# A two-layer hybrid DiT block in one core: layer 1's GLA level scores issued ahead of its SSD scans, modulation steps beside the levels, and an FFN opening that begins on the first half of the tokens

## The chip, the cores and the metric

The kernel runs on one core of a Trainium2 chip. The metric is the device time of one execution in microseconds (us); lower is better. The core has a matrix engine (TensorE, in the profile PE, with its weight loads as PEld), a vector engine (VectorE, DVE), an activation engine (ScalarE, ACT), a general engine (GpSimd, POOL) and a queue that issues DMAs (SyncE, SP). Each engine works off its own instructions in order; they wait for one another by semaphores.

## The reference, cut to what matters

The input is 512 latent tokens and 256 context tokens of width 1024. Two layers follow; each mixes tokens by three head groups side by side and then applies a SwiGLU FFN. A modulation vector (shift, scale, gate, for the mixer and for the FFN) comes from a matrix `ada_w` of 1024 x 6144 per layer.

```python
for l in range(DEPTH):                                  # DEPTH = 2
    last = l == DEPTH - 1
    mod_l = (silu(c) @ ada_w[l] + ada_b[l])             # six vectors: sh1, sc1, gt1, sh2, sc2, gt2
    p_l = modulate(rms_norm(lat, norm_mix_pre[l]), sh1, sc1) @ w_in[l]
    p_c = ...                                           # the same for the context
    gla_c, gla_l = gla_mixer(...)                       # gated linear attention, decay per key channel
    ssd_c, ssd_l = ssd_mixer(...)                       # causal conv, then Mamba-2 scans
    ret_c, ret_l = retention_mixer(...)                 # rotary retention, fixed decay per head
    mixed_l = concatenate([gla_l, ssd_l, ret_l]) @ w_out[l]
    lat = lat + gt1 * rms_norm(mixed_l, norm_mix_post[l])
    h_l = modulate(rms_norm(lat, norm_ffn_pre[l]), sh2, sc2)
    lat = lat + gt2 * rms_norm(swiglu(h_l, ffn_w13[l], ffn_w2[l]), norm_ffn_post[l])
    # the context goes through the same, but not behind the mixer of the last layer
```

All scans run in both directions; the latents start from the states at the end of the context. In layer 1 only the 512 latent tokens leave the mixer.

## The kernel before, in words

**Arithmetic.** Every large product is made of three fp32r matmuls: each operand is split into a high part (a cast on ACT, line 368) and a low part (a subtraction on DVE, line 369), and hi*hi, hi*lo and lo*hi are added up in PSUM. Tokens are worked on in blocks of 128: blocks 0 to 3 are latents, 4 and 5 context.

**Order.** The program is written in order, and a planner then lays out each engine's instructions: earlier program order goes first among those that its own timing holds ready, `tc.high_priority(offset=n)` moves a region ahead by n instructions. So work whose operands come early can run ahead of its place, as far as its tiles have memory. Tiles live in pools on a left and a right stack; a pool opened after another was closed lies over its memory, and a tile then waits until the tiles under it are done (`reuse_waits="tile"`). PSUM has eight banks: `mm` (2) for projections, `px` (5) for everything else, `pa` (1) for the modulation.

**A layer, in program order.**
- Projections of the small columns (gates, dt) and the gate chain in pool `Sa` (lines 664 to 744), which leaves the cumulated GLA gates `GG`; then the convolutions, eight blocks `fb` of 128 channels with their projections (lines 746 to 780): the conv's tiles `acc`, `th` and `xf` are in pool `Sc`, opened before `Sa`.
- The SSD scans in pool `Sb` (lines 782 to 872), at high priority: `ssd_state` and `ssd_out`, mostly DVE work. They read `CB` and `xs`, the first tiles of pool `S` on the left stack.
- The projection `gqk` of GLA's q and k (lines 873 to 880), then `rk`, `rq`, `rv` (`proj_b`, line 613).
- Retention and GLA: pools `Q` and `R` on the right, `G` and `Gl` on the left (lines 971 to 973), over pool `S`. `gla_prep` (975) makes the decayed keys and queries; `gla_levels` (1004) makes the score matrix `A` of 256 tokens level by level, for seven block sizes: subtractions on DVE and POOL (1016 to 1019), an exponential on ACT (1020), a product on DVE (1021), 8 short matmuls (1028), and four masked copies on DVE (1035). `pump` (1113) issues one piece of retention (`ret_kv`, `ret_out`) behind a level. `ret_out` holds its transposed operands in one buffer (`rqT`, line 934).
- The GLA states and outputs (`gla_kv`, `gla_step`, `gla_out`, from line 1152), the projections `gr`, `rg`, `z0`, `z1`, and the output projection by block: `out_front` (1194) normalizes, gates, transposes and multiplies with `w_out`; `out_back` (1237) adds the residual and makes the FFN's input `whole`.
- The FFN's first product by Strassen's scheme on four quarters of `whole` (`b11`, `b12` are the upper 512 features of the first and second half of the tokens, `b21`, `b22` the lower ones). Its **opening** (lines 1293 to 1370) splits `b11` and `b21`, makes the sums t1 to t4, and begins NA units (3 in layer 0, 4 in layer 1) with the two products that need `b11` and `b21` alone; then `ffn_up` (1334) works off 22 units, each with weights that are loaded, combined (417 to 420) and split.
- The FFN's second product, `down` (1387), in two passes.

**Modulation.** `Ada` (line 250) is a list of steps; a step loads 512 KB of `ada_w` into `araw` (NRAW = 3 buffers, pool `adp`) and makes 4 matmuls into `pa`; every eighth step ends one of the six vectors. `ada.some(n)` issues n steps. Layer 0 has 48 steps (32 of its own, 16 for layer 1's first two vectors), layer 1 has 32. They are issued behind `rq` (6), behind `rv` (8), in each `gla_out` (4), and what is left behind the last `out_back`.

## Time and profile before

| | |
|---|---|
| time, median of 3 runs | 1884.56 us (1883.4 to 1886.07) |
| the profiled execution, its own time | 1887.56 us |
| its span, first to last instruction | 1885.8 us |
| mean granted clock of TensorE | 0.954 of full speed |
| TensorE busy | 1748.4 us, 93% of the span |
| VectorE, ScalarE, GpSimd busy | 62%, 42%, 31% |
| HBM read and written | 233.72 MB and 38.93 MB, 145 GB/s |

The profile shows one execution, 1.9 us apart from its span and 3.0 us above the median of the timed runs. Engine busy times can overlap; a share is of the whole span. The granted clock is given as a share of full speed (2.4 GHz; the other level is 1.2 GHz, 0.50). "Idle before, releaser" names what an engine last waited for.

### The profile page before, as it was taken

The page shows a single profiled execution, that of the slowest core. Times are in us where ns is not written, and L with a number is a line of the kernel's source. Part 1 is how long each engine was busy: PE and PEld are TensorE (multiplying, and loading weights), DVE is VectorE, ACT ScalarE, POOL GpSimd, SP SyncE. Part 2 cuts the span into 40 slices and gives each one's busy share as a digit, 9 for nine tenths or more (in the row PEclk, how much of TensorE's full clock was granted, in tenths as well). Part 3 has the DMA queues.
Part 4 walks back from the last instruction along what each step waited for, and adds up shares of the span by engine and source line. Part 5 has one row for each costly group of instructions (what it writes and reads, how often), then busy time and mean ns, then how long its engine had stood idle before and what let it go on. Part 6 is the DMA issues. An engine that isn't in the chain of part 4 may idle for free. (4 is left out here: it accounts for less than half of the span.)

```text
span 1885.8 us, 30347 instructions
## 1 busy us (share of the span) xinstructions
PE 1748.4 (93%) x11851; PEld 1580.3 (84%) x11851; DVE 1164.4 (62%) x1967; ACT 791.5 (42%) x1439; POOL 592.5 (31%) x584
## 2 busy tenths in 40 slices
PE   5999999999969999999999989989977879999998
PEld 3778889988859999998788777889866879999886
DVE  4576778656467655564333528677855468888445
ACT  3545344235553433332333555534423444444343
POOL 1002624114244433231422320162313236555322
PEclk8999999999979999999999899999958979999999
DMA  8535464138534333332744473445315145444653
GB/s 280 180 103 171 139 186 132 49 112 291 176 102 132 109 107 109 93 93 97 258 142 165 133 234 122 120 145 188 103 51 185 68 129 145 130 140 129 244 201 136
DMA packets 238189, 274.63 MB, mean 146 GB/s; under 512 B 14041, under 2 KB 181437, under 8 KB 238045
## 3 DMA queue, kind: packets, MB, share of 16 engines
q1 hardware_dynamic: 236832, 270.77, 44.8%
q8 instruction: 93, 1.52, 0.3%
q10 hardware_dynamic: 1212, 1.91, 0.3%
q14 instruction: 52, 0.42, 0.1%
HBM read 233.72 MB, written 38.93 MB: 145 GB/s over the span
## 5 line engine op out<-in xcount | busy, mean ns | idle before, releaser
L369 DVE TENSOR_TENSOR wlo<-raw,whi 128x1024 fp32r<-128x1024 f32 (+2 forms) x192 | 264.2, 1382 | 162.3 <-ACT whi L368 162.1
L1316 PE MATMUL px<-H,whi 128*128 128x384 f32 (+1 forms) x1408 | 309.7, 312 | 9.2 <-ACT whi L368 9.0
L368 ACT CAST whi<-raw 128x1024 fp32r<-128x1024 f32 (+2 forms) x192 | 194.1, 1018 | 236.0 <-PE px L1316 88.0
L498 PE MATMUL mm<-whi,H 128*128 128x256 f32 x1376 | 272.2, 293 | 13.3 <-ACT stg L630 6.7
L1316 PEld LDWEIGHTS px<-H,whi 128*128 128x128 f32 x1408 | 236.8, 191 | 11.2 <-ACT whi L368 11.1
L498 PEld LDWEIGHTS mm<-whi,H 128*128 128x128 f32 x1376 | 223.0, 196 | 24.9 <-ACT stg L630 9.5
L1316 PE MATMUL px<-H,wlo 128*128 128x384 f32 (+1 forms) x704 | 212.4, 311 | 0.8 <-DVE wlo L369 0.8
L498 PE MATMUL mm<-wlo,H 128*128 128x256 f32 x688 | 200.4, 291 | 0.0
L498 PE MATMUL mm<-H,whi 128*128 128x256 f32 (+2 forms) x640 | 160.9, 342 | 4.0 <-ACT xp L759 3.6
L368 ACT CAST whi<-S 128x1024 fp32r<-128x1024 f32 x88 | 73.6, 836 | 163.1 <-DVE S L419 91.5
L498 PEld LDWEIGHTS mm<-wlo,H 128*128 128x128 f32 x688 | 134.8, 196 | 1.4
L1316 PEld LDWEIGHTS px<-H,wlo 128*128 128x128 f32 x704 | 132.2, 191 | 2.0 <-DVE wlo L369 2.0
L1271 POOL TENSOR_TENSOR hidlo<-hr,hidhi 128x768 fp32r<-128x768 f32 (+1 forms) x40 | 71.3, 1785 | 191.1 <-ACT hidhi L1270 173.3
L498 PEld LDWEIGHTS mm<-H,whi 128*128 128x128 f32 (+1 forms) x640 | 109.5, 190 | 22.6 <-ACT xp L759 5.3
L498 PE MATMUL px<-whi,H 128*128 128x256 f32 x640 | 121.1, 288 | 5.2 <-DVE H L1230 3.7
L1357 POOL TENSOR_TENSOR hf<-hf,g 128x384 f32<-128x384 f32 (+1 forms) x44 | 56.6, 1287 | 219.8 <-issue 141.3
L369 DVE TENSOR_TENSOR wlo<-S,whi 128x1024 fp32r<-128x1024 f32 x88 | 92.2, 1048 | 41.3 <-ACT whi L368 41.1
L1316 PE MATMUL mm<-blo,whi 128*128 128x384 f32 (+1 forms) x328 | 103.2, 315 | 9.5 <-DVE blo L1291 9.5
L498 PEld LDWEIGHTS px<-whi,H 128*128 128x128 f32 x640 | 100.7, 192 | 12.6 <-DVE H L1230 5.2
L498 PE MATMUL mm<-H,wlo 128*128 128x256 f32 (+3 forms) x320 | 108.5, 339 | 0.0
L1392 PE MATMUL px<-wlo,hidhi 128*128 128x512 f32 x276 | 108.3, 393 | 0.0
L1316 PE MATMUL mm<-bhi,whi 128*128 128x384 f32 (+1 forms) x328 | 103.6, 316 | 4.2 <-ACT bhi L1290 3.3
(321 smaller groups left out, 4124.0 us busy)
## 6 DMA issues: line engine op xcount, KB each, us to landing
raw<-ffn_w_dram SPq DMA_DIRECT2D x99, 512.0 KB
araw<-ada_w_dram SPq DMA_DIRECT2D x96, 512.0 KB
raw<-w_in_dram SPq DMA_DIRECT2D x26, 1024.0 KB
raw<-ffn_w_dram SPq DMA_DIRECT2D x20, 1024.0 KB
hr<-hd SPq DMA_DIRECT2D x22, 768.0 KB
hr<-hd SPq DMA_DIRECT2D x22, 512.0 KB
Rt<-gd SPq DMA_DIRECT2D x40, 256.0 KB
hd<-hf SPq DMA_DIRECT2D x22, 384.0 KB
```

The source lines that it names most:

```text
L368: S.copy(hi, src)
L369: lo_engine.tensor_tensor(lo, src, hi.bitcast(F32), ALU.subtract)
L498: PE.matmul(ps, x(k), y(k), start=(k == 0 and p == 0), stop=(k == total - 1 and p == 2))
L1271: (G if q else V).tensor_tensor(lo[:, q], hr[:, q], hi[:, q].bitcast(F32), ALU.subtract)
L1316: PE.matmul(ps[:, :hn], w[x][:, k], r[y][:, k], start=first and k == 0 and p == 0, stop=k == 3 and p == 2, skip_group_check=True)
L1357: G.tensor_tensor(h1, h1, g1, ALU.mult)
L1392: PE.matmul(ps, lh[x](k), rh[y](k), start=f + k == 0 and p == 0, stop=f + k == NF - 1 and p == 2, skip_group_check=True)
```

## The change

The functions `gla_prep` and `gla_levels` move up in the file without a change of their arithmetic. In layer 1 (`last`) their pools `G` and `Gl` are opened at the start of the layer on the right stack, the projection `gqk` comes between the conv's blocks 5 and 6, and preparation and levels are issued behind the conv and ahead of the SSD scans; retention is then issued in one go. In layer 0 levels and retention stay in their place, and three modulation steps are issued with each level. In layer 1 the buffers of the modulation come from a pool `ar` that opens behind the scans. The rest is memory (NRAW 2, fewer buffers of `xw`, `y`, `kw`, `hr`; the conv's tiles in a pool `Sd` that opens after `Sa` is closed), a second buffer for `rqT`, and a new FFN opening: NA is 4 in both layers; `b11` is split block by block in `out_back`, into the memory of the constants (`cst2`) and of `araw`; all NA units first make their `b11` product, then their `b21` product; the sums t2 and t3 have their split tiles apart from t1 and t4; all low parts are made on DVE.

```diff
-    NRAW = 3
+    NRAW = 2
-        u["xbc"] = {j: w_unit("xbc", wi, 1312 + 256 * j, 256) for j in (2, 3, 0, 1)}
-        u["gqk"] = w_unit("gqk", wi, 0, 256)
+        u["xbc"] = {}
+        for j in (2, 3, 0, 1):
+            u["xbc"][j] = w_unit("xbc", wi, 1312 + 256 * j, 256)
+            if j == 2:
+                u["gqk"] = w_unit("gqk", wi, 0, 256)
-        NA = 3 if l + 1 < NL else 4
+        NA = 4
...
+        arp = adp
         Ms = mx.enter_context(pool(f"Ms{l}", side="right"))
+        gst = ctx.enter_context(ExitStack())
         gx = ctx.enter_context(ExitStack())
+        if last:
+            Gp = gst.enter_context(pool(f"G{l}", side="right"))
+            Gl = gx.enter_context(pool(f"Gl{l}", side="right"))
...
+                kw = pt(Gl, "kw", [128, TL], bufs=1 if last else 2)[:, :n]     # in gla_prep
...
+                if li >= start:                                                # in gla_levels
+                    pump()
+                if not last:
+                    ada.some(3)
...
-            with scx:
+            with scx, pool(f"Sd{l}") as Sd:
                 for fb in (4, 5, 6, 7, 0, 1, 2, 3):
+                    if fb == 6:
+                        un = get(u["gqk"])
...
-                    acc = pt(Sc, "acc", [128, T + 4], bufs=2)
+                    acc = pt(Sd, "acc", [128, T + 4], bufs=2)
...
+            if last:
+                gc = gla_prep(TL, TC, False)
+                gl = gla_prep(0, TL, True)
+                for t0 in (0, 256):
+                    gla_levels(t0, 99)
             with pool(f"Sb{l}") as Sb, tc.high_priority(offset=300):
...
-                    xw = pt(Sb, "xw", [128, 512], bufs=2)
+                    xw = pt(Sb, "xw", [128, 512], bufs=1 if last else 2)
-                    y = pt(Sb, "y", [128, 512], bufs=3)
+                    y = pt(Sb, "y", [128, 512], bufs=2)
...
-            un = get(u["gqk"])
...
+        if last:
+            arp = ax.enter_context(pool(f"ar{l}", 2))
+        ada.ap = arp
         proj_b("rk", tbs_all, to_dram(qds[l], 256, "rope"))
...
-            qT = pt(Rp, "rqT", [128, 4, 2, 128], bufs=1)
+            qT = pt(Rp, "rqT", [128, 4, 2, 128], bufs=2)
...
-        with tc.high_priority(offset=60):
-            gc = gla_prep(TL, TC, not last)
-            if not last:
+        if not last:
+            with tc.high_priority(offset=60):
+                gc = gla_prep(TL, TC, True)
                 gla_levels(TL, 99)
-            gl = gla_prep(0, TL, True)
-        gla_levels(0, 2)
-        gla_levels(256, 1)
+                gl = gla_prep(0, TL, True)
+            gla_levels(0, 2)
+            gla_levels(256, 1)
         gls.close()
         pump(100)
...
+        near, far = ("right", "left") if last else ("left", "right")
...
-        ada.some(len(ada.todo) - 12)
+        ada.some(len(ada.todo))
...
             pre_norm(nps, l, 2, tb, x, whole, pos)                              # in out_back
+            if pos < n2:
+                cs = slice(128 * pos, 128 * pos + 128)
+                S.copy(b11h[:, :, cs], whole[:, 0:4, cs])
+                for q in range(2):
+                    ks = slice(2 * q, 2 * q + 2)
+                    V.tensor_tensor(b11l[q][:, :, cs], whole[:, ks, cs], b11h[:, ks, cs].bitcast(F32), ALU.subtract)
...
         out_back(*prev)
-        ada.some(len(ada.todo))
         rx.close()
         mx.close()
-        ax.close()
...
-            for i in range(n2):
-                cs = slice(128 * i, 128 * i + 128)
-                rsplit("b11", whole[:, 0:4, cs], cs, V)
-                rsplit("b21", whole[:, 4:8, cs], cs, G)
+            def combine(i):
...
                 V.tensor_tensor(t1, b12, b11, ALU.subtract)
                 V.tensor_tensor(t2, b22, t1, ALU.subtract)
-                G.tensor_tensor(t3, b22, b12, ALU.subtract)
+                rsplit("t2", t2, cs)
+                V.tensor_tensor(t3, b22, b12, ALU.subtract)
+                rsplit("t3", t3, cs)
                 V.tensor_tensor(t4, b21, t2, ALU.subtract)
-            for i in range(n2):
-                cs = slice(128 * i, 128 * i + 128)
-                for nm, q in (("t2", 1), ("t3", 2), ("t1", 0), ("t4", 3)):
-                    rsplit(nm, tm[:, q, :, cs], cs, V)
-                rsplit("b22", whole[:, 4:8, hn + 128 * i:hn + 128 * i + 128], cs, G)
+                rsplit("b22", b22, cs)
...
-            begun = {}
+            begun = []
             for f in range(NA):
-                un = get(u["w13a"][f])
-                ps = [mm(), px()][f % 2]
-                uu = up_first(ps, un)
-                begun[f] = uu, up_gate(ps, un)
+                un = get(u["w13a"][f], 0)
+                ps = mm() if f < 2 else px()
+                up_first(ps, un, uus[f])
+                begun.append((ps, un))
+            for i in range(n2):
+                cs = slice(128 * i, 128 * i + 128)
+                rsplit("b21", whole[:, 4:8, cs], cs)
+            for f, (ps, un) in enumerate(begun):
+                up_gate(ps, un, g1s[f])
+            for i in range(n2):
+                combine(i)
+            tb_ = pt(hp, "H", [128, 4, 4, hn], F32R)
...
+            for q, nm in enumerate(("t1", "t4")):
+                rsplit(nm, t14[:, q], allsl)
...
         fx.close()
+        ax.close()
```

## Rows read from the trace of the kernel before

**Rows 1.** The page: busy times; TensorE's busy tenths and granted clock in 40 slices.

```profile
PE 1748.4 (93%) x11851; PEld 1580.3 (84%) x11851; DVE 1164.4 (62%) x1967; ACT 791.5 (42%) x1439; POOL 592.5 (31%) x584
...
PE   5999999999969999999999989989977879999998
...
PEclk8999999999979999999999899999958979999999
```

**Rows 2.** Windows, layer 1's mixer: busy time and count by engine, granted clock, DMA.

```profile
1216.00:1312.00 96.00, 90.89 (x714) 85.38 (x713) 75.64 (x159) 41.08 (x107) 50.64 (x63) 0.98 0.52 158
1312.00:1360.00 48.00, 47.22 (x428) 44.00 (x427) 38.45 (x89) 18.66 (x43) 16.61 (x28) 1.00 0.48 155
1360.00:1412.00 52.00, 39.65 (x245) 33.76 (x244) 28.81 (x78) 15.08 (x34) 5.75 (x13) 0.62 0.15 49
1412.00:1440.00 28.00, 20.59 (x115) 15.53 (x114) 17.33 (x46) 8.20 (x20) 5.85 (x6) 0.73 0.42 126
```

**Rows 3.** Timeline of PE, one retention block; in brackets idle time before, and releaser.

```profile
1399.93 1.23 PE L950 MATMUL px<-rqT 64*128 64x128 f32 x8 [1.66 <-ACT rqT L944]
```

**Rows 4.** Waits of the whole span: who waited for whom, total, times, longest.

```profile
POOL XX L1018 <- PE px L1028: 122.2, 28, 14.2
```

**Rows 5.** Timeline of DVE where the scans end and GLA's preparation begins.

```profile
1311.52 0.88 DVE L855 TENSOR_TENSOR y<-y,y 128x512 f32<-128x512 f32 x1
...
1313.66 0.95 DVE L987 TENSOR_TENSOR kw<-GG 128x256 f32<-128x256 f32 x2
```

**Rows 6.** Groups by line, GLA levels on DVE: busy, mean ns; idle before.

```profile
L1035 DVE COPY_PREDICATED A<-msk,px 128x256 f32<-128x256 uint8 x120 | 46.6, 437 | 28.0 <-PE px L1028 27.8
...
L1021 DVE TENSOR_TENSOR XX<-XX,gqk 128x512 f32<-128x512 f32 x35 | 25.3, 724 | 6.4 <-ACT XX L1020 5.6
...
L1017 DVE TENSOR_TENSOR XX<-GG 128x128 f32<-128x128 f32 x35 | 11.9, 339 | 0.0
```

**Rows 7.** Windows, layer 0's FFN opening (first two) and its steady part.

```profile
529.70:548.00 18.30, 3.74 (x19) 2.71 (x13) 13.57 (x21) 13.96 (x26) 11.41 (x9) 0.59 0.17 57
548.00:567.60 19.60, 15.24 (x71) 14.92 (x71) 15.46 (x24) 8.31 (x16) 8.81 (x4) 0.85 0.41 108
575.00:600.00 25.00, 25.00 (x146) 25.00 (x146) 17.86 (x24) 7.84 (x11) 10.39 (x8) 1.00 0.45 131
```

**Rows 8.** Timelines of SP, DVE (three rows) and PE in layer 0's opening.

```profile
538.83 16.47 SPq L405 DMA_DIRECT2D raw<-ffn_w_dram  x5
...
541.32 3.30 DVE L1303 TENSOR_TENSOR tm<-H,tm 128x512 f32<-128x512 f32 x2
...
552.40 0.68 DVE L1303 TENSOR_TENSOR tm<-H,tm 128x512 f32<-128x512 f32 x1
...
567.62 2.29 PE L1316 MATMUL px<-H,whi 128*128 128x384 f32 x6 [4.33 <-ACT whi L368]
```

**Rows 9.** Windows, layer 1's FFN opening; then POOL's first weight combination there (timeline).

```profile
1504.40:1530.00 25.60, 15.57 (x67) 13.68 (x68) 22.74 (x31) 16.83 (x32) 10.04 (x8) 0.67 0.28 83
1530.00:1545.00 15.00, 12.05 (x80) 11.83 (x80) 5.54 (x9) 4.03 (x7) 5.11 (x4) 0.77 0.67 176
...
1532.87 1.29 POOL L417 TENSOR_TENSOR S<-raw 128x512 f32<-128x512 f32 x1 [11.84 <-DMA raw<-ffn_w_dram]
```

**Rows 10.** Chain that ended last: two modulation loads in layer 1, start and us.

```profile
1425.14 3.88 DMA araw<-ada_w_dram
...
1439.64 5.10 DMA araw<-ada_w_dram
```

**Rows 11.** Windows of modulation matmuls alone (PE, PEld): layer 0, then layer 1.

```profile
410.00:535.00 125.00, 14.17 (x48) 3.84 (x48) 0.96 0.62 218
1080.00:1300.00 220.00, 13.99 (x48) 3.92 (x48) 0.97 0.50 158
```

**Rows 12.** Layer 0: end of the gate scan (DVE timeline); the conv behind it (windows).

```profile
101.06 0.39 DVE L711 TENSOR_TENSOR_SCAN dtu<-cst,dtx 16x128 f32<-16x128 f32 x1
...
110.00:158.00 48.00, 48.00 (x280) 40.95 (x280) 32.39 (x41) 21.23 (x33) 0.00 (x0) 0.97 0.33 102
```

More of the change, by code (lines that the diff above doesn't have):

```diff
@@ L644, in tile_backbone, with gla_prep @@
             proj_b("gv", tbs_all, to_dram(vds[l], 0))
+        gA = {}
+        def gla_prep(t0, n, need):
+            nb = n // 128
+            sl = slice(t0, t0 + n)
+            q, k = gqk[:, 0, sl], gqk[:, 1, sl]
+            kwt, dec, qe = [], [], []
+            for d in range(2):
+                g3 = GG[:, d, sl].rearrange("p (b t) -> p b t", t=128)
+                end = g3[:, :, 127:128] if d == 0 else g3[:, :, 0:1]
+                dc = pt(Gp, f"gdec{t0}{d}", [128, nb], bufs=1)
+                S.activation(dc, end.rearrange("p b o -> p (b o)"), AF.Exp, scale=1.0 / 16)
+                dec.append(dc)
+                kw = pt(Gl, "kw", [128, TL], bufs=1 if last else 2)[:, :n]
+                V.tensor_tensor(kw.rearrange("p (b t) -> p b t", t=128),
+                                end.to_broadcast([128, nb, 128]), g3, ALU.subtract)
+                S.activation(kw, kw, AF.Exp, scale=1.0 / 16)
+                V.tensor_tensor(kw, kw, k, ALU.mult)
+                ps = px()
+                for i in range(nb):
+                    PE.transpose(ps[:, 128 * i:128 * i + 128], kw[:, 128 * i:128 * i + 128], ident)
+                kt = pt(Gp, f"kwt{t0}{d}", [128, n], bufs=1)
+                S.copy(kt, ps[:, :n])
+                kwt.append(kt)
+                if need:
+                    qx = pt(Gp, f"qe{t0}{d}", [128, n], bufs=1)
+                    S.activation(qx, GG[:, d, sl], AF.Exp, scale=1.0 / 16)
+                    V.tensor_tensor(qx, qx, q, ALU.mult)
+                    qe.append(qx)
+            return {"kwt": kwt, "dec": dec, "qe": qe}
@@ L744, in tile_backbone @@
                 S.activation(decx, decx, AF.Exp)
[L746 removed]
+            with scx, pool(f"Sd{l}") as Sd:
                 for fb in (4, 5, 6, 7, 0, 1, 2, 3):
+                    if fb == 6:
+                        un = get(u["gqk"])
+                        for j in range(2):
+                            for t0, n in (segs_out if j == 0 else segs_all):
+                                ps = gemm_a(un, slice(128 * j, 128 * j + 128), 128, (t0, n))
+                                if j == 0:
+                                    S.mul(gqk[:, j, t0:t0 + n], ps[:, :n], 32.0 ** -0.5)
+                                else:
+                                    S.copy(gqk[:, j, t0:t0 + n], ps[:, :n])
                     if fb % 2 == 0:
@@ L856, in ssd_out @@
                     DMA.dma_start(yds[l][tsl, :], y)
-                ada = Ada(adp, [(l, kind) for kind in range(2, 6)] + ([] if last else [(l + 1, 0), (l + 1, 1)]))
+                ada = Ada(None, [(l, kind) for kind in range(2, 6)] + ([] if last else [(l + 1, 0), (l + 1, 1)]))
                 sf = sb = None
@@ L1192, in tile_backbone @@
         whole = pt(hp, "H", [128, 8, tot])
+        hn = tot // 2
+        npos = tot // 128
+        n2 = npos // 2
+        b11h = pt(adp, "cst2", [128, 4, hn], F32R, bufs=1)
+        b11l = [pt(arp, "araw", [128, 2, hn], F32R, bufs=NRAW) for _ in range(2)]
         def out_front(pos, tb):
```

196 lines of the change are left out of this document (79 added, 117 removed).

## The prediction

> **What bounds the kernel now.** I read the page's busy line first, then its forty slices [rows 1]. TensorE (PE) is busy 93% of the span; the two FFNs, about half of the time, stand at 9 in nearly every slice with a clock of 0.9 or more. There PE is the bound and the change takes no matmul away, so nothing is to be had. The slices to look at are the few below 9: the start, slice 12 (layer 0's FFN opening), and slices 30 to 33, layer 1's mixer end and FFN opening, where busy falls to 7 or 8 and the clock to 0.5 at the lowest. There PE is called busy while it works off short matmuls at a mix of its two levels (2.4 and 1.2 GHz), so a window's busy time must be multiplied by its granted clock to know how much work is in it.
>
> The windows of layer 1's mixer do that [rows 2]. While the SSD scans run (1216 to 1312) and in the 48 us behind, PE is full at 0.98 and 1.00; the next 52 us have 39.65 us of busy at 0.62, the last 28 us have 20.59 at 0.73. Work at full clock: 89.1 + 47.2 + 24.6 + 15.0 = 175.9 us of 224, so 48 us are lost, 40 of them behind 1360. What runs there is the serial chain of a level: GpSimd (POOL) alone waited 122.2 us in 28 waits for the level's matmuls [rows 4], which is over the whole span and mostly layer 0; and each retention block makes PE wait 1.66 us for its transposed operands [rows 3]. The levels stand there because they cannot begin sooner: the last scan operation on VectorE (DVE) is at 1311.52, the first of GLA's preparation at 1313.66 [rows 5]; its pools lie over memory that the scans read. By 1360 the projections that could fill PE have run out. DVE is not full in any of these windows: 75.64 + 38.45 + 28.81 + 17.33 = 160.2 of 224.
>
> **The frame.** The profiled execution took 1887.56 us by its own time, 3.0 above the median 1884.56. I sum against the first and take 3.0 off at the end.
>
> **Layer 1's mixer, plus 25 (bounds 8 and 45).** The levels' work is unchanged and moves ahead of the scans. Its DVE part per level is four masked copies of 0.437, a product of 0.724 and two subtractions, one of them 0.339 and the other taken as the same [rows 6]: 3.15 us, for 14 levels 44 us; with some 5 us of preparation (an estimate from the 0.95 us operations [rows 5]) 49 us. The scans' stretch has 96 - 75.6 = 20.4 us of DVE free, so if all of it is used the scans end 29 us later, near 1341; the projections that now fill PE there are then left for behind it, and the 52 us at 0.62 are mixed with them. The most that can come back is the 27.4 us lost in 1360 to 1412, some of the 13 lost in 1412 to 1440, and the few us of 1216 to 1360: 45 in all. The chain states, output, norm, first modulation of the FFN stays as long as it is, so I keep its 13 lost. The least: DVE's 49 us all go on the path where PE's work is short, and only the 8 us of a half of the retention waits and some filling are left. I take 25, near the 27.4 of that one window, less what the later scans cost. The second buffer of the rotated operands is in it: its 1.66 us per block mostly lie beside other work once projections are there to fill.
>
> The wait that is added: the modulation's buffers in layer 1 now come from memory of the scans, so all 32 loads wait until about 1341 instead of 24 steps (two records each) being done before 1300 [rows 11]. SP's queue holds them in order ahead of later loads. One load took 3.88 and 5.10 us, back to back on the chain that ended last [rows 10]; with two buffers 32 of them take 62 to 82 us, to 1403 to 1423. The step that the first output block needs is the 24th, at 1388 to 1402; that block's norm is now at about 1420 and would be at 1395. So it is close, and I put 0 to 10 us of it into the 25.
>
> The Trainium skill ("DMA: Bandwidth & Descriptors", Specifications) puts a core's share of HBM at about 358 GB/s; by that, an estimate, the 16.8 MB of 32 loads would take some 47 us and nothing would wait. The loads here are paced by their 3.88 to 5.10 us in two buffers, and no run so far shows the page's rate; by it the term would be some 5 us higher.
>
> **Layer 0's FFN opening, plus 15 (5 and 22).** From the end of the last output product (529.7) to the first main product (567.62) pass 38 us [rows 7, 8]. At full clock PE's work there is 3.74 x 0.59 + 15.24 x 0.85 = 15.2 us, so 22.8 are lost. What sets the end: DVE's sums took 3.30 us for two while POOL worked beside it against 0.68 for one alone, and SP's queue stood 16.47 us at the weight loads whose memory lay over the modulation's [rows 8]. Behind it, PE waited 4.33 us for a weight's high part [rows 8]. After the change the b11 parts are ready as the blocks come, the sums are at 0.68 instead of 1.65, weights sit elsewhere, and four units instead of three can fill: 24 matmuls each at 25.00 / 146 = 0.171 us [rows 7] are 4.1 us a unit, so one more unit is not to be done later. DVE's split, sums and splits, 13.57 + 15.46 = 29.0 us before with its slow ones and some weights [rows 7], would be about 21, and the first main product comes at 549 to 552. That makes 15.6 to 18.6 earlier, less a little for POOL's work put on DVE: 15. If the main product still waits for the last sum, 5; all of it, 22.
>
> **Layer 1's FFN opening, plus 9 (0 and 16).** In 40.6 us [rows 9] the work is 15.57 x 0.67 + 12.05 x 0.77 = 19.7 us; 20.9 lost. DVE is busy 22.74 of the first 25.6, so it is the bound, and only the splits of b11 (done in the blocks before) and of POOL's slowing leave it. Behind it, POOL waited 11.84 us for a weight [rows 9], which the new place of the weights takes away if it is memory. Nine: the first main product some 10 us sooner, one lost to more work on DVE.
>
> **Layer 0's convolutions, minus 2 (-8 and +4).** The conv's tiles now lie over the gate chain's, so the first waits for its last scan at 101.06 [rows 12]. Behind that DVE is busy 32.39 of 48, 15.6 free, and PE 48 of 48 [rows 12]; what waits is taken up in the slack, and the projection gqk, now early, keeps PE full. No row shows the wait itself: half of the free 15.6 is my worst, a gain of 4 if PE's work comes better spread.
>
> **Layer 0's modulation beside the levels, minus 3 (-10 and 0).** 24 steps cost 14.17 us of PE in 410 to 535 [rows 11]; they move ahead, so their sum is nothing, but with two buffers a step can wait 3.88 to 5.10 us for its load [rows 10], and PE holds the level's matmuls behind it. Two such waits in the open cost 10, none 0.
>
> **The rest, 0.** Fewer buffers of the scans' outputs and of the FFN's halves, and one more early load of 512 KB: all are beside 93% PE [rows 1]; if their cover were gone, each is a wait of one load or one scan operation, 1 to 5 us, which is inside the bounds above.
>
> Sum: 25 + 15 + 9 - 2 - 3 = 44. 1887.6 - 44 - 3.0 = 1840.6, so **1841**. The lows and highs of the terms do not fall together; half of each side, 10 + 7 + 8 + 5 = about 20, gives its own range, 1822 to 1862.
>
> **Rivals.** *The levels and the scans only change places* (0.20): both use DVE and the same five banks px. If the levels' exponential, product and copies push the scans out by the whole 49 us, the 20.4 us of free DVE are not found, and the projections are used up while the levels run, then a stretch of scans takes the place of the one at 0.62. For it: PE was already 90.89 of 96 there [rows 2], so PE has little room either. Against it: DVE's total is 160 of 224. The mixer then gives 3, the openings 18 of 24, and the losses of 5 stay: 16, so 1868.
>
> *All terms near their upper ends* (0.09): the scans fill all of DVE's idle time and PE stays at its upper level: 45 + 22 + 16 = 83, less 8 because they hardly all fall together, 1809.
>
> *PE stands at the modulation steps* (0.12), the side that is slower: the 32 steps come after the scans, PE takes its instructions in order, and if the steps stand in its order ahead of the projections and run back to back, each waits for its load: 5.10 / 2 = 2.55 us less its own 14.17 / 24 = 0.59, so 32 x 1.96 = 63 us. With the other terms kept, 1841 + 63 = 1904. It decides from the point where more than some 22 of the 32 steps stand in the open (44 / 1.96). For it: they are issued behind rq and rv in program order, and those are just the products meant to fill PE. Against: 24 of them, issued in the same places, now cost no more than their 13.99 us [rows 11].
>
> *Nothing changes* (0.03): PE at 93% is the engine at its limit and the gaps only move, 1884. The Trainium skill ("Perfetto Trace Analysis", Identifying the Most-Contended Engine) says to improve the engine with the highest occupancy; that is PE, and the change removes no matmul. The rows on the clock, 0.59 and 0.62 [rows 2, 7], show why I weigh it low.
>
> **How the numbers follow.** The forecast itself holds 0.56. The range reaches to the exchange of places above and to the near end of the high case below, 1812 to 1876, and leaves out the slower rival, no change and half of the high ends. About 0.2%, 3.8 us, is what a measurement of this kernel can tell from none. Faster by more: 0.56 + 0.20 + 0.09 = 0.85; within: 0.03; slower: 0.12.
>
> **What would show it.** In layer 1, the first masked copies of the levels before the last scan operation, and the scans' end near 1341 on the old scale; no window of 50 us with a clock of 0.62 behind them. POOL's waits for the level's matmuls shorter. In layer 0 the first main FFN product about 20 us behind the last output product instead of 38, and DVE's sums at 0.7 us each. PE's waits for modulation loads stay below 10 us in all. The prediction is wrong if PE's idle time moves to those loads, if the scans end past 1360, or if the openings keep their 38 and 41 us with another engine last.

## The result: 3.3% slower

The changed kernel takes 1949.27 us in the median (1942.48 to 1950.43), the kernel before 1884.56: a ratio of 1.0331 with an interval of 1.031 to 1.0352, where 0.977 was forecast. Below, a run's distance from the kernel before is its ratio, less one, times 1885 us, so that each is taken against the runs on its own chip; the change is at +62.

The page after, in the form of [rows 1]: busy times of TensorE, its busy tenths in 40 slices, and the granted clock in the same slices.

```profile
PE 1780.3 (91%) x11851; PEld 1597.3 (82%) x11851; DVE 1160.4 (60%) x1981; ACT 795.3 (41%) x1433; POOL 565.9 (29%) x569
...
PE   5999999978988999999899989999668969999898
...
PEclk8999999956999999999999899999877979999999
```

TensorE has the same 11851 matmuls and 32 us more of busy time: they ran at a lower clock. The two slices of 0.5 and 0.6 lie at 390 to 487 us, in layer 0, whose levels were not to be touched. In layer 1 the slice of 0.5 is gone, and in its place stand two with busy 6. Windows of layer 0 there (columns as in [rows 2]):

```profile
336.00:384.00 48.00, 45.41 (x433) 37.12 (x431) 18.97 (x50) 10.86 (x25) 6.25 (x13) 1.00 0.67 210
384.00:432.00 48.00, 39.67 (x263) 32.70 (x260) 28.55 (x79) 10.73 (x26) 7.00 (x14) 0.64 0.18 58
432.00:480.00 48.00, 40.19 (x188) 33.41 (x187) 25.35 (x61) 16.62 (x37) 9.20 (x12) 0.61 0.18 55
```

At full clock the last two hold 39.67 x 0.64 + 40.19 x 0.61 = 49.9 us of work in 96. It is the stretch that [rows 2] showed in layer 1, with 0.62: levels and retention without a projection beside them. Layer 0 has it now because its projections are done at 395 while the levels are not. The groups by line (shortest, median and longest duration in ns; first and last start in us) give the ends of the levels in both layers, of layer 1's scans and retention, and the main FFN products:

```profile
L709 PE MATMUL px<-XX x336: 269/372/578, 306.9 to 465.3; 32*128 32x128 f32 x168
...
L1344 PE MATMUL px<-H,whi x704: 334/334/687, 604.1 to 912.4; 128*128 128x384 f32 x176
...
L709 PE MATMUL px<-XX x224: 269/270/578, 1268.0 to 1317.6; 32*128 32x128 f32 x112
...
L954 DVE TENSOR_TENSOR y<-y,y x4: 679/692/693, 1363.3 to 1407.7; 128x512 f32<-128x512 f32 x4
...
L1043 PE MATMUL px<-rqT x32: 272/272/579, 1438.6 to 1457.1; 64*128 64x128 f32 x32
...
L1344 PE MATMUL px<-H,whi x704: 274/283/579, 1589.1 to 1806.5; 128*128 128x256 f32 x176
```

In the kernel before, the first main product of layer 0 is at 567.62 ([rows 8]) and layer 1's last scan operation at 1311.52 ([rows 5]); its groups give the last level of each layer and layer 1's main products:

```profile
L1028 PE MATMUL px<-XX x336: 270/270/372, 288.9 to 411.2; 32*128 32x128 f32 x168
...
L1028 PE MATMUL px<-XX x224: 270/270/578, 1330.3 to 1410.3; 32*128 32x128 f32 x112
...
L1316 PE MATMUL px<-H,whi x704: 274/283/582, 1537.4 to 1753.5; 128*128 128x256 f32 x176
```

So 36.5 us of the loss are there at layer 0's first main product, 15 more come until layer 1's, and 10 more behind it (from 1537.4 to the end at 1885.8 were 348.4 us, from 1589.1 to 1947.5 are 358.4).

Why the levels of layer 0 are late is seen around 371 us (timelines of TensorE, VectorE and GpSimd; in brackets the idle time before, and the releaser):

```profile
341.52 0.69 DVE L702 TENSOR_TENSOR XX<-XX,gqk 128x512 f32<-128x512 f32 x1 [0.45 <-ACT XX L701]
...
370.88 0.38 PE L226 MATMUL px<-cst,araw 128*128 128x128 f32 x2
371.19 0.73 PE L709 MATMUL px<-XX 32*128 32x128 f32 x14
...
373.36 0.40 POOL L699 TENSOR_TENSOR XX<-GG 128x128 f32<-128x128 f32 x1 [34.87 <-PE px L709]
```

A level's product is done at 342.2, its matmuls run at 371.19, right behind the transposes (L226) that end a modulation vector. Between them TensorE works off, in its order, projections (23.4 us) and the eight steps of that vector, which stand among them (some 5 us). It is idle for only 1.5 us, at one load. It spends what was to be the cover, and GpSimd, and with it the next level, waits 34.87 us.

Layer 0's opening kept the wait that was to go. The rows are from the timelines of SP, GpSimd and VectorE, the last from SP's waits at 576 to 592 us (total, times, longest):

```profile
575.39 22.97 SPq L405 DMA_DIRECT2D raw<-ffn_w_dram  x6
...
599.63 1.30 POOL L417 TENSOR_TENSOR S<-raw 128x512 f32<-128x512 f32 x1 [22.62 <-DMA raw<-ffn_w_dram]
...
589.64 2.35 DVE L369 TENSOR_TENSOR wlo<-raw,whi 128x1024 fp32r<-128x1024 f32 x2
...
SPq L405 <- DVE wlo L369: 11.1, 1, 11.1
```

SP issues six weight loads over 22.97 us, where [rows 8] showed five over 16.47, and the first main product waits for these weights. But the second load comes 15.5 us behind the first, and the longest wait in between, 11.1 us, is for the low part of the weights before (`wlo`), which VectorE makes at 589.64, behind 9 us of the opening's sums and splits in its order. So the weights waited for the engine that makes the sums. In the kernel before, the profile puts SP's longest wait at this place (8.3 us) down to the same line, so the wait in [rows 8] was for the most part not one for the modulation's memory.

### The profile page after: what moved, and what is told of

Its sections match the earlier page's. It is cut to its first block, busy times and chain, and to the rows that moved or that the text cites. A ratio compares the mean times of both kernels' runs of the same rounds, so it can differ in the third digit from the quotient of the medians.

```text
span 1947.5 us, 30341 instructions
## 1 busy us (share of the span) xinstructions
PE 1780.3 (91%) x11851; PEld 1597.3 (82%) x11851; DVE 1160.4 (60%) x1981; ACT 795.3 (41%) x1433; POOL 565.9 (29%) x569
## 5 line engine op out<-in xcount | busy, mean ns | idle before, releaser
L501 PE MATMUL mm<-whi,H 128*128 128x256 f32 x1376 | 276.1, 295 | 11.3 <-ACT stg L638 6.5
L1344 PEld LDWEIGHTS px<-H,whi 128*128 128x128 f32 x1408 | 236.6, 191 | 12.1 <-ACT whi L368 11.6
L1427 PE MATMUL px<-whi,hidhi 128*128 128x512 f32 x276 | 108.9, 395 | 0.0
L501 PE MATMUL mm<-H,wlo 128*128 128x512 f32 (+3 forms) x320 | 108.7, 340 | 0.0
L1427 PE MATMUL px<-whi,hidlo 128*128 128x512 f32 x276 | 106.2, 389 | 0.0
```

Source lines behind the costliest of these rows:

```text
L501: PE.matmul(ps, x(k), y(k), start=(k == 0 and p == 0), stop=(k == total - 1 and p == 2))
L1344: PE.matmul(ps[:, :hn], w[x][:, k], r[y](k), start=first and k == 0 and p == 0, stop=k == 3 and p == 2, skip_group_check=True)
L1427: PE.matmul(ps, lh[x](k), rh[y](k), start=f + k == 0 and p == 0, stop=f + k == NF - 1 and p == 2, skip_group_check=True)
```

## The experiments

### Which part costs: steps, levels, or what is left

The four runs are the change without its steps beside the levels, without its levels ahead, without both, and the kernel before with the steps beside alone.

```diff
 # e1: the change, with
-                if not last:
-                    ada.some(3)
 # e2: the change, with layer 1 as layer 0: G, Gl on the left, levels behind the scans,
 #     two xw and kw, near and far as in layer 0
-            if last:
-                gc = gla_prep(TL, TC, False)
-                gl = gla_prep(0, TL, True)
-                for t0 in (0, 256):
-                    gla_levels(t0, 99)
-            arp = ax.enter_context(pool(f"ar{l}", 2))
 # e3: e1 and e2 together
 # e4: the kernel before, with
+                if not last:
+                    ada.some(3)
```

> The changed kernel without the three modulation steps per level in layer 0; they go back to where they were issued before (behind each GLA output and at the end). Theory A (the steps beside the levels cost layer 0 its time: the last level's matmuls went from 411 to 465 us and the first main FFN product from 567.6 to 604.1): the last level comes back to about 415, the first main product to 555 to 570, and the time falls by 35 to 50 us to 1900 to 1915. Theory B (the smaller buffers and the conv tiles laid over the gate chain cost it): the last level stays past 445 and the time stays above 1935.

Measured: 1977.07 us, 1.0477 (1.0456 to 1.0499). Theory A said 1900 to 1915, so it fell, and B's 1935 was passed by more than B explains. The last level did come back, to 417.9 us, but the first main product went to 628.4. The steps are good for something where they are; taking them away costs 27.5 us.

> The changed kernel with layer 1's levels back behind the scans, in the pools of the kernel before, and the layer's modulation buffers in their old pool; layer 0 and the FFN openings as changed. Theory C (in layer 1 scans and levels only changed places, and the stretch without projections is now the scans' end and the waits for modulation loads): layer 1 gets shorter by 5 to 20 us, 1930 to 1945. Theory D (levels ahead are worth what was forecast, and what layer 1 lost comes from elsewhere): layer 1 gets longer by 10 to 30 us, 1960 to 1980.

Measured: 1930.46 us, 1.0229 (1.0211 to 1.0247), 19 us below the change: C.

> Both undone: what is left of the change is the new FFN opening, the memory that it needs, the earlier projection gqk and the second operand buffer of retention. If A and C hold and the two parts add up: 1885 to 1900, near the kernel before. If the memory costs by itself (B): 1915 or more. If the opening gains what was forecast (24 us) and the rest costs nothing: 1855 to 1870.

Measured: 1959.57 us, 1.0385 (1.0348 to 1.0421). That lies in B's range (1915 or more), but it is not what B meant, a price of memory by itself. What I had taken for a small rest costs 73 us. Its trace says where: TensorE's timeline, the first matmul of some steps:

```profile
500.45 0.64 PE L203 MATMUL pa<-araw,sil 128*32 128x256 f32 x1 [1.06 <-DMA araw<-ada_w_dram]
...
503.23 0.64 PE L203 MATMUL pa<-araw,sil 128*32 128x256 f32 x1 [1.69 <-DMA araw<-ada_w_dram]
...
505.85 0.64 PE L203 MATMUL pa<-araw,sil 128*32 128x256 f32 x1 [1.54 <-DMA araw<-ada_w_dram]
...
508.60 0.64 PE L203 MATMUL pa<-araw,sil 128*32 128x256 f32 x1 [1.67 <-DMA araw<-ada_w_dram]
```

From 461 to 515 us TensorE does nearly nothing but steps: it is busy 19.6 of 54 us at a granted clock of 0.53, 17.2 of them with steps, one each 2.6 to 2.8 us at the end, each waiting for its load, and the first output product stands behind all of them. It must: b11's low part takes the memory of the load buffers, and it is written in the first output blocks, so that no step may be left by then.

> The kernel before with one line added: three modulation steps issued with each level of layer 0 (three load buffers as before). Theory A: the last level moves from 411 to 440 or later and the time rises by 20 to 45 us, 1905 to 1930. If the steps only hurt together with two load buffers: within 5 us of 1885.

Measured: 1907.14 us, 1.0096 (1.0069 to 1.0123), +18, just inside A's range. The last level starts at 426.0 us instead of 411.2, 14.8 later for 14.17 us of matmuls [rows 11], and the first main product at 582.1, 14.5 later; A's other sign, a last level at 440 or later, did not come. The stretch from which the steps were taken gave nothing back. The windows of that stretch, which ends where the opening of the first main product begins, in the kernel before (with the 24 steps) and in e4 (without them):

```profile
412.00:529.70 117.70, 112.50 (x952) 98.88 (x951) 62.78 (x136) 61.95 (x130) 37.26 (x38) 0.97 0.64 222
...
427.00:544.00 117.00, 103.48 (x794) 99.44 (x792) 67.84 (x135) 63.01 (x134) 34.88 (x36) 0.96 0.38 125
```

In the kernel before TensorE looked full here, at 0.97. Yet with 14 us of its work gone, the stretch is as long as before and TensorE is idle for more of it: the steps had filled time in which it would have waited for other engines. The stretch that took the steps had no such time: TensorE was busy 127.20 of the 127.20 us from 284 to 411.2 in the kernel before.

### The forced steps and the third buffer

```diff
 # f1: the kernel before, with
-        ada.some(len(ada.todo) - 12)
+        ada.some(len(ada.todo))
 # f2: the kernel before, with
-    NRAW = 3
+    NRAW = 2
 # f3: e3, with 12 steps left behind the last output block, and b11 split behind them
-        ada.some(len(ada.todo))
+        ada.some(len(ada.todo) - 12)
...
         out_back(*prev)
+        ada.some(len(ada.todo))
+        (b11h, b11l made here from whole, no longer in out_back)
 # f4: e1 with the same edit
```

> The kernel before with one number changed: no modulation steps are left for behind the last output block, all are issued ahead of the output products (three load buffers as before). Theory L (what costs layer 0 its time is that the opening's b11 low part lies in the load buffers, so that every step must be done before the first output product, and the steps run there at the pace of their loads): 12 more steps per layer stand ahead of the outputs at some 2.0 to 2.7 us each less the 0.6 of their own work, 10 to 25 us per layer, 1900 to 1930. Theory M (memory: overlays and single buffers cost it): no change, 1882 to 1890.

Measured: 1906.69 us, 1.0114 (1.0076 to 1.0151), in theory L's range, but not layer by layer, where L put 10 to 25 us in each: layer 0's first main product comes at 605.6, 38 us late, but from there to the end it is 19 us less than before.

> The kernel before with two modulation load buffers instead of three. If two buffers alone explain part of the loss: 1895 to 1910. If they only hurt where the steps stand together (theory L): within 6 us of 1885.

Measured: 1908.55 us, 1.0111 (1.0087 to 1.0136). So one buffer less costs 21 us by itself. The waits of the steps' matmuls in layer 0, 410 to 560 us (total, times, longest), in f2 and in the kernel before:

```profile
PE pa L203 <- DMA araw<-ada_w_dram: 17.4, 6, 4.4
...
PE pa L203 <- DMA araw<-ada_w_dram: 0.9, 1, 0.9
```

TensorE now stands at loads which the third buffer had let begin sooner. One reservation belongs here and to every run of this section: the order of each engine's instructions is laid out anew for each kernel, and TensorE's differs between f2 and the kernel before in many places. A price is that of the edit with its new order.

> The run without steps beside the levels and with layer 1's levels back, and in addition b11 split behind the last output block, so that 12 steps can be left for behind it as in the kernel before. What stays of the change is the rest of the opening and its memory. Theory L: the 55 us at 461 to 515, where the steps stand one behind the other ahead of the first output product, shrink; layer 0's first main product comes at 555 to 575 instead of 629.7, the time is 1875 to 1900. Theory M: it stays above 1925.

Measured: 1917.27 us, 1.016 (1.0132 to 1.0189). 42 us come back by leaving 12 steps behind; layer 0's first main product is at 581.8. Both are above L's ranges; two buffers and the rest are what is left to explain it.

> As the run before this one, with layer 1's levels ahead of the scans as in the change (and the layer's load buffers behind the scans). So it shows the price of the headline step by itself, without the steps beside and without b11 in the load buffers. If scans and levels only change places and the loads start late: 8 to 25 us above the run before. If the levels ahead gain once the steps needn't be done before the outputs: 10 to 25 us below it.

Measured: 1926.96 us, 1.0215 (1.0191 to 1.024), 10 us above f3: the levels ahead lose here too.

### The opening, the early gqk, the overlay

```diff
 # g2: f3, with
-    NRAW = 2
+    NRAW = 3
-            qT = pt(Rp, "rqT", [128, 4, 2, 128], bufs=2)
+            qT = pt(Rp, "rqT", [128, 4, 2, 128], bufs=1)
 # g2b: g2, with gqk behind the scans, acc, th and xf in Sc, three y buffers (the kernel before and the opening)
 # g3: f3, with
+        if last:
+            arp = ax.enter_context(pool(f"ar{l}", 2))
 # g4: the kernel before, with
-        ada.some(len(ada.todo) - 12)
+        ada.some(len(ada.todo) - (0 if last else 12))
 # h1: g2b with acc, th and xf in pool Sd;  h2: g2b with gqk between conv blocks 5 and 6
 # h3: g2b with the edit of g4
```

> The run with steps left behind the last output block and layer 1's levels in their old place, now with three load buffers as in the kernel before (retention's operand buffer goes back to one to make room). Two buffers cost the kernel before 21 us; if that price is the same here, the time falls from 1917 to 1890 to 1902. If two buffers cost nothing more in this frame, it stays at 1910 to 1920.

Measured: 1913.91 us, 1.0139 (1.011 to 1.0168). In this frame the third buffer (against retention's second operand buffer, which makes room for it) is worth only 4 us, within the intervals of nothing.

> As the run before this one, but with the projection gqk and the convolutions' tiles back in their places: the kernel before with nothing but the new FFN opening (four units in layer 0, b11 split behind the last output block). If the opening gains in layer 0 what the two-buffer runs suggest (66.5 us from the last output transpose to the first main product down to 56.8, and 4.2 for the fourth unit): 1868 to 1880. If the early gqk and the overlaid conv tiles are not what costs layer 1 some 13 us before its scans: no difference from the run before this one.

Measured: 1885.00 us, 0.9989 (0.9973 to 1.0006). Neither of the two cases came. The opening by itself, with `b11` split behind the last output block, is no measurable change, and the early gqk with the overlay and one `y` buffer less costs 28 us.

> The run with 1917 us (levels in the old place, steps left behind, two buffers) with one difference: layer 1's load buffers come from the pool that opens behind the scans, so that its loads wait for the scans' end as in the change. If the late loads are what the levels ahead cost in layer 1 (the run with levels ahead stood 10 us higher): 1924 to 1932. If the exchange of scans and levels is what costs: 1914 to 1920.

Measured: 1916.02 us, 1.0151 (1.0127 to 1.0176), no different from f3. Load buffers that open behind the scans cost nothing as long as the scans end where they did.

> The kernel before with layer 1's steps all issued ahead of its output products, layer 0 as it was (12 left behind the last output block). In the run that did so in both layers, layer 0 lost 38 us up to its first main product and layer 1 won 19 from there to the end. If these belong to their layers: 1865 to 1876, faster than the kernel before. If layer 1's 19 us came from what layer 0 had done: 1883 to 1895.

Measured: 1881.18 us, 0.996 (0.9942 to 0.9978): less than the expected gain, but a version that beats both kernels, the one before by 7.5 us. From layer 1's first output transposes to its first main product it takes 90.9 us instead of 96.9, without 12 steps among the output products.

> The kernel before with the new FFN opening (1885 us), and the convolutions' tiles in a pool that opens behind the gate chain's, as in the change; gqk in its old place. Together with the early gqk this cost 29 us. If the overlay is what costs (every convolution's DVE work waits for the gate chain's last scan, and what follows comes later): 1900 to 1916. If it is the early gqk: 1882 to 1890.

Measured: 1906.29 us, 1.0099 (1.0069 to 1.013), +21 against g2b.

> The other half: the same frame (1885 us) with the projection gqk between the convolutions' blocks 5 and 6, and the convolutions' tiles in their old pool. If the early gqk is what costs (some 14 us of TensorE's work put ahead of the convolutions that the scans wait for): 1898 to 1916. If it is the overlay: 1880 to 1890. If both only cost together: near 1885 here and in the run before.

Measured: 1913.82 us, 1.0146 (1.0106 to 1.0185), +30 against g2b. So each half costs about what both cost together; they do not add up. The ends of layer 0's scans, first in the frame (g2b):

```profile
L934 DVE TENSOR_TENSOR y<-y,y x5: 676/692/871, 179.6 to 276.5; 128x512 f32<-128x512 f32 x5
```

and with the early gqk (h2):

```profile
L944 DVE TENSOR_TENSOR y<-y,y x5: 680/693/872, 201.1 to 290.1; 128x512 f32<-128x512 f32 x5
```

13.6 us later; with the overlay (h1) it is 290.1 as well, with both (g2) 288.1. It looks like one delay that either half brings. Its size is near what h2's expectation puts down for gqk's matmuls, but h1 has it without them. The first main product of layer 0 is then 12.1 us late in h2, 22.0 in h1 and 20.1 in g2; why more than the delay is lost in the latter two is not settled.

> The two parts that did not lose, together: the kernel before with the new opening, and layer 1's steps all ahead of its output products (5 us better by itself). If they add up: 1874 to 1882. If the opening needs layer 1's last steps behind the outputs to fill its gap: 1882 to 1890.

Measured: 1881.45 us, 0.9974 (0.9956 to 0.9992). The time lies in the first case's range, but it is not below g4's: the opening adds nothing to g4.

### The headline step by itself

```diff
 # h4: g2b, and in layer 1 alone: G, Gl on the right, gqk early, Sd, levels ahead of the scans,
 #     the pool ar behind the scans, two load buffers, near/far swapped, one xw and kw, two y
 # i1: h4, and i2: g2b, with
-            self.todo = [(l, kind, kb) for l, kind in tasks for kb in range(8)]
+            self.todo = [(l, kind, kb) for l, kind in tasks
+                         for kb in ((0, 7) if l and kind > 1 else range(8))]
```

> The headline step by itself: the same frame (1885 us) with layer 0 untouched (three load buffers, gqk and convolutions in their old places) and, in layer 1 alone, the levels ahead of the scans with all that they need: gqk early, the overlay, two load buffers that open behind the scans. Forecast of the prediction for this step: 25 us less, 1855 to 1865. Theory C (levels and scans change places, and 32 loads begin at the scans' end): 1885 to 1905.

Measured: 1909.55 us, 1.0125 (1.0099 to 1.0152): 25.6 us above g2b and some 5 above theory C's range. Windows of layer 1's mixer in g2b, whose layer 0 ends within 2 us of h4's:

```profile
1210.00:1310.00 100.00, 95.70 (x754) 90.19 (x753) 80.14 (x166) 42.44 (x108) 53.73 (x65) 0.98 0.55 166
1310.00:1360.00 50.00, 45.75 (x415) 42.30 (x415) 40.42 (x98) 23.02 (x54) 14.41 (x26) 1.00 0.39 127
1360.00:1400.00 40.00, 33.83 (x166) 28.53 (x167) 17.94 (x48) 5.58 (x13) 3.63 (x8) 0.50 0.08 27
```

and in h4, with the ends of its levels, scans and retention by line:

```profile
1210.00:1310.00 100.00, 94.31 (x798) 87.18 (x797) 64.35 (x171) 32.56 (x65) 43.31 (x71) 0.95 0.31 92
1310.00:1360.00 50.00, 43.07 (x302) 40.99 (x301) 41.40 (x90) 29.72 (x84) 17.05 (x14) 0.90 0.44 140
1360.00:1400.00 40.00, 18.88 (x127) 11.46 (x125) 13.41 (x29) 2.45 (x8) 10.94 (x15) 0.70 0.57 194
...
L712 PE MATMUL px<-XX x224: 270/270/578, 1231.1 to 1282.2; 32*128 32x128 f32 x112
...
L956 DVE TENSOR_TENSOR y<-y,y x4: 680/693/693, 1327.9 to 1372.5; 128x512 f32<-128x512 f32 x4
...
L1054 PE MATMUL px<-rqT x32: 272/272/373, 1403.7 to 1419.0; 64*128 64x128 f32 x32
```

VectorE is busy 64.35 of the first 100 us, 80.14 in the frame. The levels did not fill the scans' gaps, they put the scans off: the last scan operation is at 1372.5 against 1305.8. The cause can be seen in the timelines of GpSimd and TensorE: the scans' first operand (`xw`), the last level, the scans' first state product.

```profile
1216.41 1.22 POOL L891 TENSOR_TENSOR xw<-xs,wcol 128x512 f32<-128x512 f32 x1
...
1281.73 0.74 PE L712 MATMUL px<-XX 32*128 32x128 f32 x16
...
1287.91 1.02 PE L895 MATMUL px<-xw,bt 128*128 128x256 f32 x4
```

The operand was there at 1217.6, but in TensorE's order the scans' first products stand behind all levels; in the frame the first of them is at 1215.1. So nothing of the scans could run between the levels, however much of VectorE was free. The change has the same order (1251.69, 1317.16, 1323.33). Whether another order, with the scans' products among the levels, would have gained was not tried.

In the frame the retention was done among the levels (1359.9 to 1398.2); now it comes behind the scans, at 1403.7 to 1419.0. The stretch at half clock has become 40 us with 18.88 x 0.70 = 13.2 us of work, against 33.83 x 0.50 = 16.9. The first output transposes are then 1 us later than in the frame, counted from layer 0's last first-product matmul (568.2 against 567.2 us), the outputs take 65.5 us instead of 48.9, and from the first main product to the end it is 6.4 us more.

TensorE's waits for modulation loads in layer 1, 1120 to 1700 us, in h4 and in g2b:

```profile
PE pa L203 <- DMA araw<-ada_w_dram: 22.0, 12, 6.2
...
PE pa L203 <- DMA araw<-ada_w_dram: 3.5, 2, 3.1
```

This run holds more than the levels: the early gqk, the overlay and the two buffers, which layer 1 needs for them, are not in g2b. In f4 against f3, which both have these, the scans end 49.3 us later (1386.9 against 1337.6) and the price is 10 us.

> The headline step by itself (1909.6 us) with work left out: of the eight modulation steps of each of layer 1's four vectors made in layer 1 only the first and the last are done (8 loads instead of 32; the vectors are then sums over a quarter of the input). To be read against the next run, which leaves out the same. If the headline's 24 us come from the 32 loads that begin at the scans' end: 0 to 10 us above the next run. If they come from the exchange of levels and scans itself: 18 to 30 us above it. If the forecast's mechanism is right once the loads are gone: 10 to 25 us below it.

> The frame of the headline run (the kernel before with the new opening, 1885 us) with the same steps left out, layer 1's levels behind the scans. Its 24 left-out steps of layer 1 are 14 us of TensorE's time beside other work and a few waits at the outputs: 1865 to 1882.

Measured: 1888.25 us, 0.9999 (0.9982 to 1.0016), and 1862.69 us, 0.9862 (0.9829 to 0.9895): 25.8 us apart. That is the second case; the number of late loads is not what costs. (i2 is below its own range: the 24 steps left out are worth 26 us to the frame, not their 14.) The outputs' 16.6 us are gone (44.4 us against 44.3), but then the first output transposes come 13.2 us later than in i2, and the end behind layer 1's first main product is 10.2 us longer. The run does not clear the steps altogether. In i1's timeline of TensorE the eight that are left stand between the scans' end (1368.1) and the retention, and TensorE waits 12.8 us for their loads and 6.7 for VectorE there, nearly as long as in h4:

```profile
1369.21 0.63 PE L203 MATMUL pa<-araw,sil 128*32 128x256 f32 x1 [3.24 <-DMA araw<-ada_w_dram]
...
1378.25 0.63 PE L203 MATMUL pa<-araw,sil 128*32 128x256 f32 x1 [6.69 <-DVE araw L217]
1383.72 0.63 PE L203 MATMUL pa<-araw,sil 128*32 128x256 f32 x1 [4.39 <-DMA araw<-ada_w_dram]
...
1403.21 1.28 PE L1021 MATMUL px<-vvg,rkw 128*128 128x128 f32 x8 [0.25 <-POOL rkw L1016]
```

How the loss is shared between the scans put off and the few steps that stand there is open; a run with none of them was not tried.

## Why the prediction was wrong, point by point

In the order change by change, each run against the one before it: two load buffers 20.9 (f2), then opening, early gqk, overlay and second operand buffer 9.2 (f3), then b11 in the load buffers, which forces all steps ahead of the outputs, 42.4 (e3), then the steps beside the levels, 29.4 back (e2), then the levels ahead, 19.2 (the change). The sum is 62.3. Along another way the terms have other sizes, since they overlap (the third buffer is worth 21 us in one frame and 4 in another). Five edits of the kernel before or of g2b that touch different things each cost 18 to 30 us (e4, f1, f2, h1, h2); how much of that is the order that is laid out anew, and not the edit, these runs can't say. That a new order does not cost by itself is seen in g2b, g3, g4 and h3, which are edits too and stand within 8 us of what they are compared with. The places of the loss named here are those that the traces show.

- **Layer 1's levels, plus 25.** Measured minus 25.6 with all that they need (h4 against g2b), and minus 10 to 19 in the frames that have the early gqk, the overlay and two buffers on both sides (f4 against f3, e1 against e3, the change against e2). The step that failed is an overlap: that VectorE's 20.4 free microseconds would be used, so that the scans would end 29 us later with projections left for behind them. They ended 66.7 later in h4 (49.3 in f4), because the scans' first products stand behind all levels in TensorE's order. So the scans followed the levels instead of running between them, the projections were used up meanwhile, and the 40 us behind 1360 hold 13.2 us of work. A free share of an engine in a window is not room for a second chain if another engine's order keeps the chains apart. I had named it as a rival (levels and scans only change places, 0.20), with a gain of 16 in all.
- **The added wait at the loads, 0 to 10 inside the 25.** In the change layer 1's steps run from 1408 to 1522, not to 1423, and TensorE waits 18.2 us for their loads in 11 waits; in the whole kernel its matmuls into `pa` wait 25.5 us for loads, where the prediction called more than 10 a sign of being wrong (the kernel before had 11.7). g3 says that late loads cost nothing if the scans end early, i1 that their number is not the cause. Whether waits at a few of them behind late scans are a part of it is open.
- **Layer 0's opening, plus 15; layer 1's, plus 9.** Measured plus 2, within nothing, for the opening without its early split of `b11` (g2b). In the change itself, where `b11` is split block by block, it takes 34 us from layer 0's last output product to the first main product, which was to fall from 38 to some 20, and 33 in layer 1 (34 in the kernel before). VectorE's part was right: the sums take 0.68 us each and no longer 1.65. But what sets the end was mis-named. I took the sums, with the weights "elsewhere"; it is the load of the next weights, for which GpSimd waited 22.62 us, and which itself waited for a split that VectorE makes behind the sums. And the fourth unit's 4.2 us did not show as a gain behind it: in g2b the first main product is 4.6 us sooner, the last of layer 0 only 2.9.
- **Layer 0's convolutions, minus 2 (-8 to +4).** Measured minus 28 for both layers together (g2 against g2b). The step that failed is "gqk, now early, keeps PE full". It did, but PE was full there already [rows 12], so that its matmuls went in ahead of the convolutions and of all that hangs on them (h2, minus 30). "What waits is taken up in the slack" failed as well: the overlay alone costs 21 (h1).
- **Steps beside the levels, minus 3 (-10 to 0).** Measured minus 18 alone (e4). "They move ahead, so their sum is nothing" was the failed step: 14.17 us put into a full stretch made it 14.8 longer, and the stretch from which they came did not get shorter. In the change's own frame the same edit gained 29, because the steps would otherwise stand in one lump.
- **The rest, 0.** The third load buffer was costed at 1 to 5 us; it is worth 21 in the kernel before. TensorE's 93% was no cover: its matmuls run in order, and the 17.4 us for which they stood at loads in layer 0 (f2) held back what was behind them.
- **What was not in the sum.** The change's line that issues all steps ahead of the outputs was in the diff and had no term. It costs 42 us with two buffers. The slower rival (0.12) had this mechanism and its price (2.55 us a step; e3 shows 2.6 to 2.8), but it put it only behind layer 1's scans and not ahead of the outputs, where e3 shows it in layer 0. The memory said so: the split of b11 takes the load buffers, and they must be free.
- **The range.** Its last step has a slip: 10 + 7 + 8 + 5 is 30, not about 20, so the sum's own range would have been 1811 to 1871. The measured time is far outside either way.

By the limit of about 358 GB/s for a core in the Trainium skill ("DMA: Bandwidth & Descriptors", Specifications), 32 loads would take about 47 us, an estimate. At e3's pace of 2.7 us they take some 86, with 225 GB/s moved at 461 to 515 us, so the page's rate is not what paces loads that wait for a buffer in use. It is not a ceiling for this one core either: 394 GB/s were moved in 14 us of g2b's second FFN product (1766 to 1780).

## What to carry to other kernels

Where the matrix engine is full, what is put ahead makes everything behind it later by its own length; it comes back only if the stretch that it left is bound by that engine too. A busy share does not tell: the stretch that e4 relieved was busy 112.5 of 117.7 us at 0.97 and did not get shorter. Cover is a stock: a change that moves independent work forward, or lets it run while a chain waits, must say what covers the chain later. And when a tile is laid over a buffer, look which instructions must all be done before it is written: that is a new order, and it has a price even if no wait is seen in the code.

## What the runs showed of the hardware that was not expected

- Two buffers instead of three for loads of 512 KB: TensorE's waits at them in layer 0 rose from 0.9 us (1 wait) to 17.4 us (6 waits), from 410 to 560 us.
- The loads of e3, one after the other in two buffers, come one each 2.6 to 2.8 us, a little slower than half of the longer of the two single loads seen before (5.10 / 2 = 2.55, [rows 10]).
- The stretch from layer 1's first main product to the end was 6 to 10 us longer in the runs with levels ahead (348.4 in the kernel before and 358.4 in the change, 348.5 in g2b and 354.9 in h4, 346.1 in i2 and 356.3 in i1); most of it comes behind the last first-product matmul. The runs with levels ahead have the sides of the FFN's pools swapped; whether that is the cause was not tried.
